# Two transformer blocks on one core: three column steps to one modulation step, the first mixer's norm directly behind its core, nine expert weights announced there

## The chip, the cores and the metric

The kernel runs on one core of one Trainium2 chip. The metric is the device time of one execution in microseconds, from the kernel's start to its end; several executions are timed and the median counts.

## The reference

`x` is 256 tokens by 1024 columns, `c` one row of 1024, all in float32. A first block mixes the tokens with two heads groups, then runs a mixture of experts; a second block follows (hybrid attention, two squared-ReLU MLPs, a pooling mixer). The change touches the first block, cut to what matters:

```python
mod = silu(c) @ ada_w + ada_b                       # 1024 x 6144
sh_m, sc_m, g_m, sh_f, sc_f, g_f = split(mod, 6)    # "modulation"
h = rms_norm(x, mix_norm_w) * (1 + sc_m) + sh_m
proj = h @ w_in                                     # "columns": r, k, v, lora, qk, v, o, gates
y_r = rwkv7(proj[..., :RWKV_COLS])                  # first mixer: a recurrence, then a norm per head
y_m = mlstm(proj[..., RWKV_COLS:])                  # second mixer: four heads, then a norm per head
x = x + g_m * (concat(y_r, y_m) @ w_out)
h = rms_norm(x, ffn_norm_w) * (1 + sc_f) + sh_f
x = x + g_f * moe(h)      # top group of 4, top 2 of its 8 experts; 32 experts x 3 weights of 1 MB
```

The second block starts with the same kind of modulation, from `c_2` and weights of its own.

## The kernel before

Activations lie with channels on the 128 partitions and 256 tokens along the row. A product is made of three fp32r matmuls, from a high and a low part of each operand; `split` makes the two parts of a weight, the high one on ScalarE, the low one on VectorE (line 297).

**Tiles.** Weights come through SyncE's DMA queue, in order, into 8 slots of 1 MB (tag `w`, `NWSLOT`). General work tiles of 128 x 1024 (tag `t4`) number 28 (`NT4`); three pairs `wh`/`wl` hold split weights (`NSPLIT`).

**Lanes.** The first block's work is laid out in program order by a small planner. Lane 0 holds the column products of `w_in` by name: `mg`, `r`, `v`, `mqk`, `mv`, `mo`, eight steps each apart from `mg`. Lane 1 holds the modulation loads of 1 MB each, eight a piece: `g1`, `f`, `ada00`, `gates20`, `ada01` (the last three belong to the second block). `side` is the second mixer as a generator, `mlstm_core`; it waits for `mqk` and `mv`, and asks for `mo` late. The first mixer is written straight through, `rwkv_prep`, `rwkv_core`, `rwkv_out`, and calls `fill(gap)` where TensorE would wait: one step of `side`, then steps of the lanes until the planned time `gap` is used up. A lane-1 step is taken when the planner thinks its load has come and `RATIO` lane-0 steps lie behind (line 208; `mg` and `r` go first). `need(names)` runs a lane up to a name, `more(n)` runs n lane-1 steps, `warm(n)` issues n matmuls of no use, which depend on nothing.

**Behind the core** (`run`, from line 2443): all columns and the rest of `side` are run to the end; then the gate of the first mixer, `rwkv_out` (the norm, with the half of the out projection that reads the second mixer, `pom`, as filler), ten expert loads (`E1`), `need("pom", "g1")`, the row of `g_m`, two expert loads, `need("f")`, the half of the out projection that reads the first mixer with the residual, four expert loads, then `route`. `route` runs three lane-1 steps (`R3`) and two more (`R6`), which are steps of `ada00`.

**Expert loads** (`moe_loads`, line 1738) are numbered n = 0 to 95: eight groups of four gate, four up and four down weights. The first 16 go ahead: n = 0 to 3 (from `WA`) into `w` slots, the next nine into pairs of `t4` tiles, three into the split pairs. n = 16 to 27 may take any of the three kinds that has come free, and from n = 28 (`REUSE`) only `w` slots. A load into `t4` or split tiles is two transfers of 0.5 MB, one into a `w` slot is one of 1 MB.

The program order is not the final order: the compiler's scheduler orders each engine's instructions by when it expects their operands and tiles, and that order is fixed then. On the chip each engine and each DMA queue works it off in order.

Of the kernel before, what the change touches and what calls it, by code (L numbers as in the profile page):

```python
# [45 lines left out]
SM, SO = 1, 1  # L46
PM, PO = "ada", "mm"
R1 = 0
RATIO = 2
R2 = 4  # L50
R3 = 3
R4 = 2
R5 = 0
R6 = 2
E5 = 3
GM = -1
VC = 2
WA = 0
EX = 1
CAT = (0, 1)  # L60
REUSE = 28
W1 = 4
W2 = 2
W3 = 0
# [5 lines left out]
W5 = 0  # L70
W6 = 0
N1 = 99
POS, E1, E2 = 10, 10, 2
BAND = 143

VEC_ROWS = [
# [77 lines left out]
class Net:  # L154
# [45 lines left out]

    def fill(self, gap):

        if self.side and next(self.side, None) is None:
            self.side = None
        end = self.now + gap
        while self.now < end:
            loaded = self.lanes[1] and self.vectors > 0 and self.arrival() + 2.0 <= self.now
            if self.lanes[0] and not (loaded and self.turns >= RATIO and self.lanes[0][0][0] not in self.urgent):
                self.step(0)
                self.turns += 1  # L210
            elif loaded:
                self.step(1)
                self.vectors -= 1
                self.turns = 0
            else:
                break
        self.now = max(self.now, end)

    def warm(self, n, after=None):

# [1288 lines left out]
    def route(self, ss, scale, shift):  # L1509
# [78 lines left out]
        B = small("Bm", 2, 32)  # L1588
        ohb = oh[:, :, :, None].to_broadcast([128, 2, 4, 8])
        nc.vector.tensor_mul(B.rearrange("p a (g e) -> p a g e", g=4), b8[:, :, None, :].to_broadcast([128, 2, 4, 8]), ohb)  # L1590
        self.more(R3)
        p = self.ps("ppos")
        self.mm(p[:, 0:32], self.c("striu"), B[:, 0], start=True, stop=True)
        self.mm(p[:, 32:64], self.ones, B[:, 0], start=False, stop=False, skip_group_check=True)
        self.mm(p[:, 32:64], self.c("striu"), B[:, 1], start=False, stop=True, skip_group_check=True)
        self.warm(R4)

# [9 lines left out]
        self.gather(S, 0)  # L1607
        self.more(R6)
        for _ in range(NWSLOT - 4):
# [128 lines left out]
    def moe_loads(self):  # L1738


        nc, I = self.nc, self.I
        self.moe_w = {}
        self.moe_free = {"w": NWSLOT, "t4": MOE_AHEAD - NSPLIT, "split": NSPLIT}
        for n, (kind, e) in enumerate(self.moe_order()):
            first = n < 4 + MOE_AHEAD
            order = ("w",) if WA <= n < WA + 4 else ("t4", "split") if first else ("w", "t4", "split") if n < REUSE else ("w",)
            while True:
                pool = next((o for o in order if self.moe_free[o]), None)
                self.stuck = pool is None
                if pool:  # L1750
                    break
                yield
            self.moe_free[pool] -= 1
            W = I["moe_w_" + kind][0, e]
            src = W.rearrange("(k p) n -> p k n", p=128) if kind == "down" else \
                W.rearrange("(h p j) n -> p h (j n)", h=1, j=8)
            if pool == "w":
                w = self.slot()
                if kind == "down" and e == 31:
                    for c in range(2):  # L1760
                        nc.sync.dma_start(w.rearrange("p (k c n) -> p k c n", k=2, c=2)[:, :, c],
                                          src.rearrange("p k (c n) -> p k c n", c=2)[:, :, c])
                elif kind == "down":
                    nc.sync.dma_start(w.rearrange("p (k n) -> p k n", k=2), src)
                else:
                    nc.sync.dma_start(w, src[:, 0])
                w = [w[:, 0:1024], w[:, 1024:2048]]
            else:
                if pool == "split":
                    w = [self.spool.tile([128, 1024], F32, name="we", tag=t) for t in ("wh", "wl")]  # L1770
                else:
                    w = [self.t4("we") for _ in range(2)]
                for h in range(2):
                    v = src[:, h] if kind == "down" else src[:, 0, h * 1024:(h + 1) * 1024]
                    nc.sync.dma_start(w[h], v)
            self.moe_w[kind, e] = (w, pool)
            yield
# [15 lines left out]
    def moe(self, S, consts):  # L1793
# [62 lines left out]
        for g in range(8):  # L1856
            if g == 2:
                self.overflow(S, gate, acc)
            p = self.ps("pgu")
            with self.behind(quad(g, 0, "gate", p)):  # L1860
                if last:
                    combine(g - 1, *last)
                self.slot_weights(S, g)
                if g in (5, 6):
                    residual(g - 5)
                if g == 7:
                    next(consts)
            ot, cwg = S["ot"], S["cwg"]
            with self.behind(quad(g, 1, "up", p)):
                t = act(p)  # L1870
                if g == 0:
                    self.overflow_flag(S)
                    gate = self.ada_gate(S["gate"], 1, "g_f")
                if g < 7:
                    self.gather(S, g + 1)
                if g == 5:
                    fw, fw2 = self.rows_of(self.vecs("final_norm_w"), "fw"), self.t4("fw2")
                    nc.scalar.activation(fw2, fw, AF.Square)
                last = ot, *down(g, t, cwg)
# [498 lines left out]
    def run(self):  # L2378
        nc, I = self.nc, self.I
# [6 lines left out]
        ss = self.ss()  # L2386
# [40 lines left out]
        M = {}  # L2427
# [15 lines left out]
        Y = self.rwkv_core(S)  # L2443
        self.mark("core")
        self.vectors = 99
        self.need("mg", "mqk", "mv", "mo")
        while self.side:
            self.fill(0)
        self.dump("ym", M["out"])
        self.expert_loads = self.moe_loads()  # L2450
        consts = self.attn_consts()

        def experts(n):
            for _ in range(n):
                next(self.expert_loads)

        HH, banks = [None, M["parts"]], {}
        self.later("pom", self.out_proj_half(I["w_out"][0], HH, 1, banks, True))
        S["gate"]()
        next(consts)  # L2460
        yr = self.rwkv_out(S, Y)
        self.dump("yr", yr)
        self.mark("out")
        experts(E1)
        HH[0] = self.split_act(yr)
        self.need("pom", "g1")
        self.gate = self.ada_gate(A["g1"]["m"], 0, "g_m")
        next(consts)
        experts(E2)
        self.need("f")  # L2470
        ss = self.ss()
        self.all(self.out_proj_half(I["w_out"][0], HH, 0, banks, False, ss))
        experts(4 + MOE_AHEAD - E1 - E2)
        self.dump_x("x1")
        mf = A["f"]["rows"]
# [24 lines left out]
        first = self.rsqrt(q, u)  # L2500
# [3 lines left out]
        for a in range(2):  # L2504
            n = [nc.vector.tensor_scalar(xn[a][:, 0:512], acc[a, 0], q[:, a:a + 1], None, op0=ALU.mult),
                 nc.scalar.activation(xn[a][:, 512:1024], acc[a, 1], AF.Copy, scale=q[:, a:a + 1])] if not XO else \
# [26 lines left out]
        HH = [None, self.split_act(osw)]  # L2533
        banks = {}
# [5 lines left out]
        ss = self.ss()  # L2540
# [10 lines left out]
        ss = self.ss()  # L2551
# [28 lines left out]
        ss = self.ss()  # L2580
# [5 lines left out]
        ss = self.ss()  # L2586
# [37 lines left out]
```

## Time and profile before

| | us |
|---|---|
| median of 3 timed runs | 1046.53 (1045.27 to 1047.58) |
| the profiled execution: its own time | 1038.73 |
| its span, from the first to the last instruction | 1037.1 |
| TensorE busy | 946.2 (91% of the span) |
| VectorE busy | 558.0 (54%) |
| ScalarE busy | 424.2 (41%) |
| GpSimd busy | 37.7 (4%) |
| TensorE's mean granted clock | 0.96 of full |
| read from HBM | 282.25 MB, with the writes 273 GB/s over the span |

The profile's page cuts the span into 40 slices of 25.9 us. Four stages can be told apart by the names of the matmuls: the first block's mixers to about 260 us, routing and experts to about 506, attention to about 650, then the two MLPs with the pooling mixer between them. A busy TensorE is not TensorE at its peak: the clock that it was granted has to be read beside it.

### The profile page before, as it was taken

The numbers are of one execution on the slowest core, as the hardware profiler recorded it, in microseconds if no ns is written. First come the engines' busy times: TensorE is split into PE (matmuls) and PEld (weight loads), VectorE is DVE, ScalarE is ACT, GpSimd is POOL, SyncE is SP. The second block draws the span as 40 slices with busy tenths as digits, with TensorE's granted clock in tenths as the row PEclk, the third lists the DMA queues.
The fourth block names the chain that finished last, engine by engine and source line by source line (L and its number), as shares of the span: only waits on it lengthen the run. The fifth ranks groups of instructions, "written<-read, shape, count | busy, mean of one in ns | idle before, by whom it ended". The sixth has DMA issues, their size and how long they took to land.

```text
span 1037.1 us, 18248 instructions
## 1 busy us (share of the span) xinstructions
PE 946.2 (91%) x7667; PEld 744.6 (72%) x7667; DVE 558.0 (54%) x941; ACT 424.2 (41%) x691; POOL 37.7 (4%) x53
## 2 busy tenths in 40 slices
PE   4898999989698877887899999999999999999996
PEld 1687776867474544444487677998989889999995
DVE  1477671536223221111499537898878775444446
ACT  1373334343212111021466435654444575444553
POOL 1020000001000000000000000100000010000000
PEclk9999999989689899898999999999999999999999
DMA  8998436537969999999995867799989925555501
GB/s 255 346 332 326 163 124 245 203 122 278 412 260 359 372 416 415 415 418 417 385 359 202 291 207 273 238 373 322 354 307 369 329 109 183 189 197 188 178 1 41
DMA packets 89658, 284.53 MB, mean 274 GB/s; under 512 B 10525, under 2 KB 14930, under 8 KB 77798
## 3 DMA queue, kind: packets, MB, share of 16 engines
q1 hardware_dynamic: 88106, 281.36, 73.5%
q10 hardware_dynamic: 956, 1.47, 0.4%
q8 instruction: 61, 1.00, 0.4%
q0 software_dynamic: 512, 0.52, 0.3%
q14 instruction: 23, 0.19, 0.0%
HBM read 282.25 MB, written 1.07 MB: 273 GB/s over the span
## 4 chain that ended last, share of the span: by engine, by line
PE 79%; DMA 10%; DVE 5%; ACT 3%; issue 2%; POOL 1%; SPq 1%; POOLq 0%; ACTq 0%; DVEq 0%
PE pB L181 28%; PE pm L181 17%; PE pgu L181 5%; DMA w<-in_moe_w_up_dram 4%; PE pada L457 4%; PE po L181 3%; DMA w<-in_moe_w_gate_dram 3%; PE pxg L181 3%; DMA w<-in_ada_w_dram 2%; PE pyd L181 2%; PE pacc L181 2%; PE pv L181 1%; DVE wl L297 1%; PE pgv L181 1%; DMA x<-in_x_dram 1%
## 5 line engine op out<-in xcount | busy, mean ns | idle before, releaser
L297 DVE TENSOR_TENSOR wl<-w,wh 128x1024 fp32r<-128x1024 f32 x186 | 226.9, 1225 | 124.3 <-ACT wh L296 124.2
L296 ACT CAST wh<-w 128x1024 fp32r<-128x1024 f32 x186 | 194.5, 1050 | 207.9 <-PE pB L181 98.8
L181 PE MATMUL pB<-hh,wh 128*128 128x256 f32 x800 | 219.1, 289 | 5.2 <-issue 2.8
L181 PE MATMUL pB<-hh,wl 128*128 128x256 f32 x800 | 215.7, 285 | 0.8 <-DVE wl L297 0.8
L181 PE MATMUL pB<-hl,wh 128*128 128x256 f32 x800 | 214.8, 285 | 0.8 <-DVE hl L657 0.7
L181 PEld LDWEIGHTS pB<-hh,wh 128*128 128x128 f32 x800 | 149.6, 193 | 16.6 <-issue 9.2
L181 PEld LDWEIGHTS pB<-hl,wh 128*128 128x128 f32 x800 | 149.1, 193 | 4.2 <-issue 2.9
L181 PEld LDWEIGHTS pB<-hh,wl 128*128 128x128 f32 x800 | 149.2, 193 | 3.7 <-issue 2.5
L181 PE MATMUL pm<-wh,fh 128*128 128x512 f32 (+1 forms) x262 | 101.2, 387 | 0.0
L181 PE MATMUL pm<-wl,fh 128*128 128x512 f32 (+1 forms) x262 | 100.8, 385 | 0.0
L181 PE MATMUL pm<-wh,fl 128*128 128x512 f32 (+1 forms) x262 | 100.6, 384 | 0.0
L181 PE MATMUL pgu<-w,xg 128*32 128x256 f32 x832 | 68.7, 440 | 23.3 <-DMA w<-in_moe_w_gate_dram 18.7
L181 PEld LDWEIGHTS pgu<-w,xg 128*32 128x32 f32 x832 | 31.6, 126 | 61.2 <-DMA w<-in_moe_w_gate_dram 26.2
L537 DVE SCALAR_TENSOR_TENSOR w<-w,csil 128x1024 f32<-128x1024 f32 x56 | 70.5, 1277 | 0.0
L181 PEld LDWEIGHTS pm<-wh,fh 128*128 128x128 f32 x262 | 49.1, 188 | 12.2 <-ACT fsq L2239 2.5
L181 PEld LDWEIGHTS pm<-wh,fl 128*128 128x128 f32 x262 | 49.2, 188 | 9.8
L181 PEld LDWEIGHTS pm<-wl,fh 128*128 128x128 f32 x262 | 49.3, 188 | 9.6 <-DVE wl L297 0.3
L457 PE MATMUL pada<-w,csil 128*32 128x512 f32 x256 | 43.6, 660 | 8.1 <-DMA w<-in_ada_w_dram 8.1
L2241 DVE TENSOR_TENSOR fl<-fsq,fh 128x512 fp32r<-128x512 f32 x32 | 22.0, 688 | 30.3 <-ACT fh L2240 30.3
L181 PE MATMUL pyd<-w,aT 128*32 128x512 f32 x224 | 28.9, 596 | 9.5 <-ACT aT L1819 9.5
L1654 ACT CAST slotT<-pcw 128x256 fp32r<-128x256 f32 x8 | 3.0, 373 | 78.4 <-PE pcw L181 78.4
L1625 DVE TENSOR_TENSOR oh<-cs,pos 128x256 f32<-128x256 f32 x8 | 3.4, 426 | 58.7 <-PE pcw L181 58.6
(556 smaller groups left out, 1291.0 us busy)
## 6 DMA issues: line engine op xcount, KB each, us to landing
w<-in_mlp_w_dram SPq DMA_DIRECT2D x64, 1024.0 KB
w<-in_ada_w_dram SPq DMA_DIRECT2D x40, 1024.0 KB
w<-in_ada_w_dram SPq DMA_DIRECT2D x64, 512.0 KB
w<-in_moe_w_up_dram SPq DMA_DIRECT2D x28, 1024.0 KB
w<-in_moe_w_down_dram SPq DMA_DIRECT2D x27, 1024.0 KB
w<-in_moe_w_gate_dram SPq DMA_DIRECT2D x24, 1024.0 KB
w<-in_w_in_dram SPq DMA_DIRECT2D x12, 1024.0 KB
w<-in_attn_w_in_dram SPq DMA_DIRECT2D x9, 1024.0 KB
```

What stands on the lines that cost most here:

```text
L181: return self.nc.tensor.matmul(out, lhsT, rhs, **kw)
L296: nc.scalar.copy(h, w)
L297: self.split_ins = nc.vector.tensor_sub(l, w, h)
L457: nc.tensor.matmul(acc[32 * j:32 * j + 32, :], self.csil[:, which, k:k + 1].to_broadcast([128, 32]), w[:, j * 512:(j + 1) * 512], start=(k ...
L537: nc.vector.scalar_tensor_tensor(acc[:, s], w[:, s], ck, acc[:, s], op0=ALU.mult, op1=ALU.add)
L1625: nc.vector.tensor_tensor(oh.rearrange("p a (e s) -> p a e s", s=32), self.c("slots")[:, None, None, :].to_broadcast([128, 2, 4, 32]), S[" ...
L1654: nc.scalar.copy(ot, p[:, 0:T])
L2241: nc.vector.tensor_sub(fl[:, s], sq[:, s], fh[:, s])
```

## The change

- `RATIO` goes from 2 to 3 until `mv` is done, and to 0 from then on. `fill` steps `side` once as before and then once more in every third round of its loop (new `side_step`).
- Behind the core nothing is run to its end any more. The gate, then nine expert loads (`E1` = 9), then `rwkv_out` follow at once. Only then comes `need("mo")`, and the half of the out projection that reads the first mixer is issued first, a step of it and a step of `side` by turns.
- `need("g1", "ada00")` stands ahead of the row of `g_m`; so all of `ada00` is done before the second half of the projection, which now reads the second mixer and carries the residual. Four expert loads (`E2`) stand between.
- In `route` the three and the two lane-1 steps are gone (`R6` = 0); 8 and 3 of the matmuls of no use stand in the places of `R3` and `R4`.
- `WA` = 9: the first nine expert loads go into `t4` pairs, the next four into `w` slots, three into split pairs.
- From group 2 on (`moe_big`) loads up to n = 83 (`LAST` = 84) may again take `t4` and split tiles.

```diff
--- before.py
+++ after.py
@@ -46,19 +46,19 @@
 SM, SO = 1, 1
 PM, PO = "ada", "mm"
 R1 = 0
-RATIO = 2
+RATIO = 3
 R2 = 4
-R3 = 3
-R4 = 2
+R3 = 8
+R4 = 3
 R5 = 0
-R6 = 2
+R6 = 0
 E5 = 3
 GM = -1
 VC = 2
-WA = 0
+WA = 9
 EX = 1
 CAT = (0, 1)
-REUSE = 28
+REUSE, LAST = 28, 84
 W1 = 4
 W2 = 2
 W3 = 0
@@ -70,7 +70,7 @@
 W5 = 0
 W6 = 0
 N1 = 99
-POS, E1, E2 = 10, 10, 2
+E1, E2 = 9, 4
 BAND = 143
 
 VEC_ROWS = [
@@ -200,12 +200,15 @@
 
     def fill(self, gap):
 
-        if self.side and next(self.side, None) is None:
-            self.side = None
         end = self.now + gap
+        self.side_step()
+        n, ratio = 0, 0 if "mv" in self.done else RATIO
         while self.now < end:
+            n += 1
+            if n % 3 == 0:
+                self.side_step()
             loaded = self.lanes[1] and self.vectors > 0 and self.arrival() + 2.0 <= self.now
-            if self.lanes[0] and not (loaded and self.turns >= RATIO and self.lanes[0][0][0] not in self.urgent):
+            if self.lanes[0] and not (loaded and self.turns >= ratio and self.lanes[0][0][0] not in self.urgent):
                 self.step(0)
                 self.turns += 1
             elif loaded:
@@ -215,6 +218,10 @@
             else:
                 break
         self.now = max(self.now, end)
+
+    def side_step(self):
+        if self.side and next(self.side, None) is None:
+            self.side = None
 
     def warm(self, n, after=None):
 
@@ -1588,7 +1595,7 @@
         B = small("Bm", 2, 32)
         ohb = oh[:, :, :, None].to_broadcast([128, 2, 4, 8])
         nc.vector.tensor_mul(B.rearrange("p a (g e) -> p a g e", g=4), b8[:, :, None, :].to_broadcast([128, 2, 4, 8]), ohb)
-        self.more(R3)
+        self.warm(R3)
         p = self.ps("ppos")
         self.mm(p[:, 0:32], self.c("striu"), B[:, 0], start=True, stop=True)
         self.mm(p[:, 32:64], self.ones, B[:, 0], start=False, stop=False, skip_group_check=True)
@@ -1740,10 +1747,11 @@
 
         nc, I = self.nc, self.I
         self.moe_w = {}
+        self.moe_big = False
         self.moe_free = {"w": NWSLOT, "t4": MOE_AHEAD - NSPLIT, "split": NSPLIT}
         for n, (kind, e) in enumerate(self.moe_order()):
             first = n < 4 + MOE_AHEAD
-            order = ("w",) if WA <= n < WA + 4 else ("t4", "split") if first else ("w", "t4", "split") if n < REUSE else ("w",)
+            order = ("w",) if WA <= n < WA + 4 else ("t4", "split") if first else ("w", "t4", "split") if n < REUSE or self.moe_big and n < LAST else ("w",)
             while True:
                 pool = next((o for o in order if self.moe_free[o]), None)
                 self.stuck = pool is None
@@ -1856,6 +1864,7 @@
         for g in range(8):
             if g == 2:
                 self.overflow(S, gate, acc)
+                self.moe_big = True
             p = self.ps("pgu")
             with self.behind(quad(g, 0, "gate", p)):
                 if last:
@@ -2443,33 +2452,35 @@
         Y = self.rwkv_core(S)
         self.mark("core")
         self.vectors = 99
-        self.need("mg", "mqk", "mv", "mo")
-        while self.side:
-            self.fill(0)
-        self.dump("ym", M["out"])
         self.expert_loads = self.moe_loads()
         consts = self.attn_consts()
 
         def experts(n):
             for _ in range(n):
                 next(self.expert_loads)
-
-        HH, banks = [None, M["parts"]], {}
-        self.later("pom", self.out_proj_half(I["w_out"][0], HH, 1, banks, True))
         S["gate"]()
+        experts(E1)
         next(consts)
         yr = self.rwkv_out(S, Y)
         self.dump("yr", yr)
         self.mark("out")
-        experts(E1)
-        HH[0] = self.split_act(yr)
-        self.need("pom", "g1")
+
+        HH, banks = [self.split_act(yr), None], {}
+        self.need("mo")
+        po = self.out_proj_half(I["w_out"][0], HH, 0, banks, True)
+        while self.side:
+            next(po, None)
+            self.side_step()
+        self.all(po)
+        self.dump("ym", M["out"])
+        HH[1] = M["parts"]
+        self.need("g1", "ada00")
         self.gate = self.ada_gate(A["g1"]["m"], 0, "g_m")
         next(consts)
         experts(E2)
         self.need("f")
         ss = self.ss()
-        self.all(self.out_proj_half(I["w_out"][0], HH, 0, banks, False, ss))
+        self.all(self.out_proj_half(I["w_out"][0], HH, 1, banks, False, ss))
         experts(4 + MOE_AHEAD - E1 - E2)
         self.dump_x("x1")
         mf = A["f"]["rows"]
```

## Rows read from the trace of the kernel before

**Rows 1.** The page: GB/s of all DMA in 40 slices of the span

```profile
GB/s 255 346 332 326 163 124 245 203 122 278 412 260 359 372 416 415 415 418 417 385 359 202 291 207 273 238 373 322 354 307 369 329 109 183 189 197 188 178 1 41
```

**Rows 2.** Chain that ended last, whole span: start us, us, what

```profile
358.62 12.88 DMA w<-in_moe_w_up_dram
...
477.78 14.36 DMA w<-in_moe_w_up_dram
```

**Rows 3.** Windows: length; busy PE, PEld, DVE, ACT, POOL; PEclk; DMA share, GB/s

```profile
210.00:240.00 30.00, 27.23 (x150) 19.52 (x149) 11.15 (x23) 11.48 (x20) 5.76 (x5) 0.83 0.30 106
240.00:260.00 20.00, 19.79 (x115) 15.20 (x114) 15.96 (x31) 7.74 (x14) 1.86 (x3) 1.00 0.97 374
260.00:270.00 10.00, 1.86 (x7) 0.49 (x5) 2.11 (x5) 1.22 (x5) 1.60 (x2) 0.75 1.02 413
270.00:290.00 20.00, 18.51 (x74) 14.83 (x74) 5.64 (x34) 4.13 (x8) 0.43 (x2) 0.50 0.92 365
290.00:300.00 10.00, 9.19 (x99) 6.19 (x102) 2.64 (x9) 1.51 (x4) 0.00 (x0) 0.88 0.40 154
...
320.00:350.00 30.00, 25.76 (x298) 17.03 (x297) 7.01 (x19) 4.52 (x11) 0.00 (x0) 0.94 0.84 331
...
370.00:480.00 110.00, 86.04 (x778) 47.25 (x778) 22.30 (x51) 16.61 (x38) 0.00 (x0) 0.92 1.02 416
```

**Rows 4.** Windows of 10 us, same columns

```profile
200.00:210.00 10.00, 10.00 (x128) 8.71 (x127) 6.86 (x24) 3.78 (x6) 0.73 (x1) 1.00 0.49 190
...
230.00:240.00 10.00, 10.00 (x55) 8.55 (x54) 2.70 (x5) 3.56 (x5) 3.59 (x3) 1.00 0.01 2
```

**Rows 5.** Timeline of SyncE's queue, 160 to 282: start us, us, issue

```profile
185.95 17.54 SPq L1766 DMA_DIRECT2D w<-in_moe_w_gate_dram  x4
...
217.83 22.17 SPq L445 DMA_DIRECT2D w<-in_ada_w_dram  x2
240.06 4.77 SPq L1775 DMA_DIRECT2D we<-in_moe_w_up_dram  x8
246.44 9.86 SPq L1775 DMA_DIRECT2D we<-in_moe_w_down_dram  x8
257.25 0.33 SPq L445 DMA_DIRECT2D w<-in_ada_w_dram  x1
```

**Rows 6.** Waits of SyncE's queue, 200 to 300: us, times, longest

```profile
SPq L445 <- DVE wl L297: 21.5, 1, 21.5
```

**Rows 7.** Timeline of TensorE, routing: start us, us, group, count [idle before <-releaser]

```profile
259.82 0.28 PE L181 MATMUL po<-wh,yl 128*128 128x256 f32 x1
...
268.69 1.91 PE L457 MATMUL pada<-w,csil 128*32 128x512 f32 x2 [8.14 <-DMA w<-in_ada_w_dram]
...
281.71 1.93 PE L457 MATMUL pada<-w,csil 128*32 128x512 f32 x6
...
287.63 6.07 PE L181 MATMUL pxg<-oh,xp 128*128 128x128 f32 x32
293.62 1.92 PE L457 MATMUL pada<-w,csil 128*32 128x512 f32 x16
...
296.95 3.23 PE L181 MATMUL pgu<-w,xg 128*32 128x256 f32 x56
```

**Rows 8.** Timeline of TensorE, from the core's end to the projection

```profile
210.23 0.68 PE L181 MATMUL pyi<-Pm,Z 64*64 64x64 f32 x16
...
223.18 2.15 PE L436 MATMUL pbc<-cs,rb 128*128 128x128 f32 x8 [1.99 <-DVE rb L431]
...
228.04 1.88 PE L181 MATMUL pc<-Y,first 128*128 128x512 f32 x4
...
248.78 0.50 PE L181 MATMUL po<-wh,yh 128*128 128x512 f32 x1
```

**Rows 9.** Chain that ended last, a later gather

```profile
347.97 3.78 PE pxg L181 x32
...
353.60 3.76 PE pyd L181 x32
```

## The prediction

> **What bounds the kernel now.** I read the chain that ended last first, then the busy time by windows, then the queue of SyncE and TensorE's timeline where the chain names them.
>
> In the experts' stage the chain is held five times by an expert weight's transfer, 12.5 to 15.5 us each, 69.8 us together [rows 2]. The page shows why: the transfers run at 415 to 418 GB/s in five slices on end [rows 1], and 416 over 110 us [rows 3]. No window shows clearly more for long, so this stage ends when its bytes are in. It can end earlier only if bytes move before it.
>
> Before it they could. From 210 to 300 us five windows move 106 x 30 + 374 x 20 + 413 x 10 + 365 x 20 + 154 x 10 = 23.6 MB [rows 3]; at 416 GB/s that is 56.8 us, so 33.2 us of transfer time are lost. The worst stretch is 230 to 240 with 2 GB/s [rows 4]. SyncE's queue says what it waited for: four gate weights took slots from 186 to 203, and a modulation load then sat 21.5 us until a split freed a slot [rows 5, 6]. The twelve loads into work tiles stood behind it in the queue and came at 240 [rows 5].
>
> Their late start hits back in routing. A load of `ada00` issued at 257.25 queues behind sixteen halves of expert weights, and TensorE, whose fixed order has this step between two transposes, stands 8.14 us until 268.69 [rows 5, 7]. The granted clock is 0.50 over the next 20 us [rows 3], which is its lower level, 1.2 of 2.4 GHz.
>
> In the core itself there is little to win: TensorE is busy 10.00 of 10 us from 200 to 210 at full clock [rows 4].
>
> **Part by part.**
>
> *The three lane-1 steps in `route` go.* They are the groups at 268.69, 281.71 and 293.62 [rows 7]. (1) The stall: 8.1 us. (2) The first step itself, 1.9 us at half clock. (3) The last one: the gather ends at 293.7, the experts' first matmul starts at 296.95, 3.25 us later; in a later group the same pair is 1.85 us apart (351.75 to 353.60) [rows 9]. Gain 1.4 us. (4) The gather itself took 6.07 us, and 3.78 at a better clock [rows 7, 9]: 2.3 us, or nothing if the clock falls all the same. (5) From 270.6 to 281.2 lie transposes and router products at half clock, 10.6 us; between nothing and 5.3 us; I take 3, since part of it waits for copies. The middle step (281.71, 1.93 us) lies beside VectorE's top-k and costs nothing now. Sum 16.7 us, between 11.4 (without 4 and 5) and 19.0.
>
> *The matmuls of no use*, 8 and 3, stand where TensorE waits for VectorE (from 283.6, where the step of 281.71 ends, to the next product); they depend on nothing and cost 0, at most the 1 us by which eight of them outlast that wait at half clock, which I leave in the range.
>
> *The three steps come earlier*, 16 matmuls of two steps took 1.92 us [rows 7], so 2.9 us more before the projection's second half. Their loads move with them, ahead of the split-pair loads on SyncE's queue.
>
> *The norm directly behind the core.* Now TensorE waits there for the second mixer's norm (1.99 us at 223.18 [rows 8]); from 210 to 240 it is idle 2.8 us, and at a mean clock of 0.83 about 10.2 us run at the lower level [rows 3]. Full cover gains at most 2.8 + (10.2 - 2.8) / 2 = 6.5 us. Against it: the norm's chain, from 228.04 to the first product with its result at 248.78, is 20.7 us long [rows 8], and now one half of the projection runs under it. A half is 11.3 us (248.78 to 260.1 [rows 7, 8]). In the change both halves follow the chain, and under it lie the rest of `mo`, of the modulation (eight steps of 0.96 us for `ada00` alone) and the last of the second mixer. With the 2.9 us, the bounds are a gain of 6.5 - 2.9 = 3.6 and a loss of 11.3 - 3.6 = 7.7. TensorE's work is the same in sum, and the planner kept it at 10.00 of 10 with the same fillers [rows 4], which is nearer the good end; I take 0.
>
> *Ratio 3, then 0, and more steps of `side`.* The order changes, the sum of the work does not, and TensorE is full either way [rows 4]. 0, and what shifts here is inside the bounds above.
>
> *Nine loads announced at the core, none in a slot.* They need no weight slot, so neither they nor the slots' users wait as at 217.83 [rows 5]. They cost TensorE nothing and SyncE 18 issues of 0.33 us. The price of being late or early is in the transfers: if the experts start 16.7 us earlier, the same 23.6 MB must come in 73.3 us, 322 GB/s. The windows at 240 to 270 show 374 and 413 [rows 3], so there is room.
>
> *Work tiles and split tiles reused up to n = 83.* At full rate deeper buffers give nothing. From 320 to 350 the rate is 331 [rows 3], and this is 30 x (1 - 331 / 416) = 6.1 us of transfer time; most of it lies before group 2. 0 to 2.5, I take 1. Against this part speaks what the Trainium skill says in "DMA: Bandwidth & Descriptors", Rules for kernel authors: transfers of at least 1 MiB for full bandwidth, and these loads are cut in two. By the fit in its section on the anatomy of one DMA (2.0 us and the bytes over 436 GB/s, given for GpSimd's path) two halves would take 6.4 us and a whole 4.4; an estimate for 56 loads with nothing overlapped is 112 us more, and the sum would be a loss. Here eight halves were issued in 9.86 us [rows 5] while the windows, filled with such halves, moved 374 and 413 GB/s [rows 3]. The trace disagrees with the rule, since the fixed part overlaps, and I give it no chance of its own.
>
> **Sum.** 16.7 + 0 + 1 = 17.7 us, taken one to one from the end of the experts' stage, since it is bound by transfers that start that much earlier, and from there to the end, where TensorE's work is unchanged. The profiled span 1037.1 becomes 1019.4; its own time of 1038.73 lies 7.8 below the median of 1046.53, and I carry the difference over: 1046.5 - 17.7 = 1028.8. The terms' bounds give a gain of 3.7 to 25.1, the lost transfer time of 33.2 us is the outer limit.
>
> **The rivals.**
>
> *The norm is held by tiles.* Nine loads are eighteen of 28 work tiles, asked for ahead of the norm's own. Where the second mixer and `mo` still hold theirs, the norm waits, its chain starts where it does now, and a whole half of the projection comes uncovered behind it: 11.3 us back, a gain of 6.4, 1040.1. For it: the twelve loads came only at 240. Against: the wait named there is for a weight slot [rows 6].
>
> *The wait for `ada00` moves.* Its last loads queue behind nine expert weights, and TensorE stands ahead of the projection's second half instead of in routing. The stall, the step and the half clock come back there: 8.1 + 1.9 + 3 + 2.3 = 15.3 us, a gain of 2.4, 1044.1. For it: this is what happened at 257.25 behind the same loads [rows 5]. Against: the slots are free, so the loads can be issued sooner.
>
> *The transfers give it all back.* The experts start earlier, but the loads before do not come earlier, and the chain's waits of 12.5 to 15.5 us grow by as much: no change, 1046.5. For it: the stage is bound by bytes [rows 2]. Against: 230 to 240 at 2 GB/s [rows 4] was for want of slots.
>
> *Slower: the queue is blocked in the experts' stage.* With up to n = 83 on work and split tiles, SyncE's fixed order puts loads for different tiles in one line; a load whose tile comes free late holds those whose slots are free, and the rate falls. At the 331 GB/s of 320 to 350 the bytes of the 110 us from 370 to 480 take 138.2 us [rows 3]: 28.2 us more, 1057. It decides from 358 GB/s down, where the loss is 17.7. Against: up to twenty buffers instead of eight.
>
> **How the numbers follow.** The forecast has 0.55, tiles 0.15, `ada00` 0.12, given back 0.08, blocked queue 0.10. A measurement of this kernel can tell about 0.2% from no change, 2.1 us. Faster: 0.55 + 0.15, half of the 0.12 and a little of the 0.08, 0.78; within: 0.10; slower: 0.10 and a little, 0.12. The range leaves out the blocked queue and what is given back, and reaches from the forecast's best bound with some of the 33.2 us beyond it, 1016, to the moved wait, 1045.
>
> **What would show it.** No modulation matmul between the projection's last product and the experts' first, and about 20 us between these two instead of 37.1. The clock in routing above 0.8. A first load into work tiles at about 212 and over 300 GB/s from 215 to 240. The experts' first product at about 280, their last at about 489, with five waits still near 14 us. If the first load into work tiles is still near 240, or the norm's first product near 228, the tiles hold it; a wait for a modulation load ahead of the row of `g_m` is the second rival; a rate under 400 in the middle of the experts' stage is the slower one. I am wrong altogether if the core itself ends at another time than now (its last product stands at 210.23 [rows 8]), since I gave its new order nothing.

## The result: 1.1% slower

The changed kernel takes 1057.99 us (median, 1055.03 to 1058.87), the kernel before 1046.3 beside it: a ratio of 1.0106, interval [1.0083, 1.0129]. The forecast was 1028.8. The profiled execution of the changed kernel took 1057.74 us, span 1056.1, so the two traces lie 19.0 us apart, and the readings below add up to 19.0. Some 7 of these are no cost of the change: the trace of before is of an execution 7.8 us quicker than its median, as the prediction says.

| us from the span's start, TensorE | before | after | later by |
|---|---|---|---|
| first mixer's core, begin of its last product group | 210.23 | 229.81 | 19.6 |
| norm's first product `pc` | 228.04 | 232.25 | 4.2 |
| first projection product with the norm's result | 248.78 | 263.40 | 14.6 |
| begin of the last projection product | 259.82 | 291.92 | 32.1 |
| first expert product | 296.95 | 310.46 | 13.5 |
| end of the last expert product | 508.03 | 521.24 | 13.2 |
| end of TensorE's last product | 1029.11 | 1048.14 | 19.0 |

So the routing does what was forecast: from the last projection product to the first expert product it takes 18.5 us instead of 37.1. Everything ahead of it is 32.1 us late, and the attention behind the experts loses another 5.8: from the last expert product to the first product of the first MLP it is 168.0 us instead of 162.2.

The line numbers of after are those of before plus 7 from about line 220 on and plus 8 from about 1750 on; in the other kernels they shift by other amounts, and the names tell what is meant. TensorE's timeline of after from the core's end to the experts, for [rows 7, 8] (start us, us, group, count, idle before and releaser):

```profile
220.02 0.68 PE L181 MATMUL pyi<-Pm,Z 64*64 64x64 f32 x16
...
229.81 0.68 PE L181 MATMUL pyi<-Pm,Z 64*64 64x64 f32 x16
...
234.06 6.21 PE L464 MATMUL pada<-w,csil 128*32 128x512 f32 x56
240.21 1.09 PE L443 MATMUL pbc<-cs,rb 128*128 128x128 f32 x8
...
256.52 1.11 PE L443 MATMUL pbc<-cs,rb 128*128 128x128 f32 x4 [10.35 <-DVE rb L438]
261.53 1.11 PE L443 MATMUL pbc<-cs,rb 128*128 128x128 f32 x4 [3.90 <-DVE rb L438]
263.40 0.79 PE L181 MATMUL po<-wh,yh 128*128 128x512 f32 x1 [0.75 <-ACT yh L1223]
...
291.92 0.28 PE L181 MATMUL po<-wh,yl 128*128 128x256 f32 x1
...
305.10 5.43 PE L181 MATMUL pxg<-oh,xp 128*128 128x128 f32 x32 [0.32 <-DVE b L1621]
310.46 1.91 PE L181 MATMUL pgu<-we,xg 128*32 128x256 f32 x29
```

Two things stand out. Between the core's last two products (220.02, 229.81) lies nearly 9 us of other work: 71 products `pB` in single rows, the second mixer's projection `mo`, which its core asks for with `need("mo")` in the middle of the first mixer's chain. And the norm's `pbc` products wait 10.35 and 3.90 us for a copy `rb`. VectorE's timeline of after says what that copy stood behind:

```profile
226.05 0.75 DVE L542 TENSOR_SCALAR w<-w,csil 128x1024 f32<-128x1024 f32 x1 [2.96 <-DMA w<-in_ada_w_dram]
...
253.42 1.28 DVE L544 SCALAR_TENSOR_TENSOR w<-w,csil 128x1024 f32<-128x1024 f32 x1 [8.43 <-DMA w<-in_ada_w_dram]
...
256.04 0.42 DVE L438 COPY rb<-hr 128x512 f32<-128x512 f32 x1
256.37 1.28 DVE L544 SCALAR_TENSOR_TENSOR w<-w,csil 128x1024 f32<-128x1024 f32 x1
...
261.05 0.42 DVE L438 COPY rb<-hr 128x512 f32<-128x512 f32 x1
```

Lines 542 and 544 are the running sum of `gates20`, a modulation that only the attention wants, some 300 us later. The planner, at none to one, has begun it, and its product at 253.42 waits 8.43 us for its load. The copy's own input is there by about 247, when GpSimd's `hr` ends. The load of `gates20` is behind 18 halves of expert weights on SyncE's queue, whose timeline answers to [rows 5]:

```profile
223.19 4.47 SPq L1783 DMA_DIRECT2D we<-in_moe_w_gate_dram  x8
229.10 10.63 SPq L1783 DMA_DIRECT2D we<-in_moe_w_up_dram  x8
240.69 1.62 SPq L1783 DMA_DIRECT2D we<-in_moe_w_down_dram  x2
243.25 4.09 SPq L452 DMA_DIRECT2D w<-in_ada_w_dram  x4
248.34 1.66 SPq L728 DMA_DIRECT2D w<-in_w_out_dram  x2
```

The windows of after, for [rows 3, 4] (length; busy PE, PEld, DVE, ACT, POOL; PEclk; DMA share, GB/s):

```profile
230.00:240.00 10.00, 10.00 (x84) 4.26 (x80) 2.77 (x7) 4.03 (x9) 0.00 (x0) 1.00 1.02 411
...
250.00:260.00 10.00, 1.11 (x4) 0.71 (x4) 6.57 (x11) 0.00 (x1) 0.00 (x0) 0.50 1.03 398
...
320.00:330.00 10.00, 9.54 (x106) 6.22 (x109) 3.50 (x8) 4.00 (x9) 0.00 (x0) 1.00 0.35 120
...
370.00:480.00 110.00, 73.23 (x723) 41.96 (x724) 19.23 (x47) 14.35 (x32) 0.00 (x0) 0.83 1.02 412
```

The transfers did come early, 411 GB/s at 230 to 240 where there had been 2. But from 250 to 260 TensorE works 1.11 of 10 us, and at 320 to 330, in the midst of the experts, the transfers fall to 120 GB/s, where before they had 294.

### The profile page after: what moved, and what is told of

It is laid out like the page before. It is cut to its first block, busy times and chain, and to the rows that moved or that the text cites. A ratio compares the mean times of both kernels' runs of the same rounds, so it can differ in the third digit from the quotient of the medians.

```text
span 1056.1 us, 18325 instructions
## 1 busy us (share of the span) xinstructions
PE 935.5 (89%) x7676; PEld 744.7 (71%) x7676; DVE 560.5 (53%) x941; ACT 423.4 (40%) x691; POOL 37.4 (4%) x53
## 4 chain that ended last, share of the span: by engine, by line
PE 50%; DMA 10%; DVE 2%; issue 2%; ACT 1%; POOL 0%; SPq 0%; POOLq 0%; ACTq 0%; DVEq 0%
PE pB L181 20%; PE pm L181 16%; PE pgu L181 3%; DMA we<-in_moe_w_up_dram 2%; PE po L181 2%; DMA we<-in_moe_w_gate_dram 2%; DMA w<-in_moe_w_gate_dram 2%; DMA w<-in_moe_w_up_dram 1%; PE pyd L181 1%; DMA w<-in_moe_w_down_dram 1%; PE pgv L181 1%; DMA w<-in_ada_w_dram 1%; DMA we<-in_moe_w_down_dram 1%; PE pacc L181 1%; PE pada L464 1%
## 5 line engine op out<-in xcount | busy, mean ns | idle before, releaser
L181 PE MATMUL pgu<-w,xg 128*32 128x256 f32 x528 | 39.8, 416 | 27.9 <-DMA w<-in_moe_w_gate_dram 25.6
L181 PEld LDWEIGHTS pgu<-w,xg 128*32 128x32 f32 x528 | 19.6, 120 | 48.1 <-DMA w<-in_moe_w_gate_dram 27.4
L464 PE MATMUL pada<-w,csil 128*32 128x512 f32 x256 | 38.0, 661 | 0.0
L1840 DVE SCALAR_TENSOR_TENSOR mg<-pyd,slotw,g_f 128x512 f32<-128x512 f32 x16 | 12.0, 749 | 45.6 <-PE pyd L181 42.5
L181 PEld LDWEIGHTS pxg<-oh,xp 128*128 128x128 f32 x256 | 30.8, 201 | 3.2 <-issue 2.5
```

Of the source, the lines that this page charges most:

```text
L181: return self.nc.tensor.matmul(out, lhsT, rhs, **kw)
L464: nc.tensor.matmul(acc[32 * j:32 * j + 32, :], self.csil[:, which, k:k + 1].to_broadcast([128, 32]), w[:, j * 512:(j + 1) * 512], start=(k ...
L1840: nc.vector.scalar_tensor_tensor(yg[:, s], py[c], cwg, gate[:, s], op0=ALU.mult, op1=ALU.mult)
```

## The experiments

From here every run is compared with runs of the kernel before on its own chip, by ratio: there before had medians of 1043.8, 1043.7 and 1041.8 us, and single executions between 1035.1 and 1049.0. "MB issued" is added up from SyncE's queue; the expert weights are 100.7 MB in all. The theories were these. A: the planner's new order makes the first mixer's core late. B: the early `gates20` holds the norm on VectorE. C: the early expert weights do, on SyncE's queue. D: none to one goes on in the attention. E: a begun `gates20` keeps a weight slot through the experts' stage. F: what the early expert weights take is large slots, and `ada00` lacks them.

### The two halves of the change alone

`e3_planner_only`, on the kernel before:

```
-RATIO = 2
+RATIO = 3
...  fill(): the changed one, with n % 3 and ratio 0 behind "mv"
```

> The kernel before with the new planner alone (three to one, then none to one once the second mixer's v columns are done; its core stepped at every third step): tail, routing and loads as before. Theory A: the core ends about 20 us later; the second mixer's steps that stood between core and norm (17.8 us from 210.23 to 228.04) are gone, so the net is +2 to +10 us, and with gates20 ahead of the norm up to +20: 1049 to 1066 us. Rival (the planner helps and the tail is at fault): 1030 to 1043 us.

Measured: 1073.94 us, ratio 1.0312 [1.0259, 1.0365], worse than A's upper end. The core ends 14 us late and the experts begin 13 us late, their stage takes another 12 us more, and from there to the end it is 6 us more.

`e4_routing_only`, on the kernel before:

```
-R3 = 3
-R4 = 2
+R3 = 8
+R4 = 3
...
-R6 = 2
+R6 = 0
...
-        self.more(R3)
+        self.warm(R3)
...
-        self.need("pom", "g1")
+        self.need("pom", "g1", "ada00")
```

> The kernel before with the routing part alone: ada00 is finished ahead of the first gate, the five modulation steps in the routing become eight warming products there, none at its end. The sum of the prediction for this part: -16.7 us, 1029.8 us, with the stretch from the last projection product to the first expert product at about 20 us instead of 37.1. Rival 1 (the 47 us of ada00's steps move ahead of the second projection half and cost there what they cost here): 1040 to 1046 us. Rival 2 (the experts' stage is bound by its loads at 416 GB/s, which do not start earlier): the first expert product comes 15 us earlier, the last one at the same time, 1044 to 1047 us.

Measured: 1039.29 us, ratio 0.9970 [0.9946, 0.9995], 3.1 us. That is Rival 1, 0.7 us below its range. The routing is some 17 us long, and ahead of it TensorE's timeline shows the stall that was taken out of it:

```profile
259.63 1.94 PE L457 MATMUL pada<-w,csil 128*32 128x512 f32 x8 [15.72 <-DMA w<-in_ada_w_dram]
...
294.96 3.66 PE L181 MATMUL pgu<-w,xg 128*32 128x256 f32 x64
```

The step that in routing waited 8.14 us [rows 7] waits 15.72 us ahead of the first gate, and the experts begin 2 us earlier than before. So moving the steps is worth next to nothing as long as their loads come when they come.

### Where the planner's loss lies

`e1_gates_late`, on the changed kernel:

```
-            loaded = self.lanes[1] and self.vectors > 0 and ...
+            loaded = self.lanes[1] and self.lanes[1][0][0] not in self.held and self.vectors > 0 and ...
...
-        R["gate"] = A["g1"]["m"]
+        R["gate"], self.held = A["g1"]["m"], ()
```

with `held` at first `("gates20", "ada01")`.

> The changed kernel, in which the two later modulations gates20 and ada01 may not start before the routing is done. Theory B (VectorE's queue: the products of gates20 wait for their loads and hold the norm's small copies rb behind them): the two TensorE gaps of 10.35 and 3.90 us ahead of the norm's pbc go, the first projection product moves from 263.4 us to 249-254 us, and of the 5.7 us lost in the attention stage some come back: 1038 to 1046 us. Theory C (the nine early expert weights fill SyncE's queue and hold the loads that the norm's neighbours need): the gaps stay under another name, 1055 to 1060 us. By either the core ends where it does in the changed kernel, 229.8 us.

Measured: 1045.73 us, ratio 1.0019 [0.9990, 1.0049]; the changed kernel had 1.0106. For the norm B holds. TensorE's timeline:

```profile
243.46 1.06 PE L443 MATMUL pbc<-cs,rb 128*128 128x128 f32 x4
244.91 1.12 PE L443 MATMUL pbc<-cs,rb 128*128 128x128 f32 x4 [0.39 <-DVE rb L438]
249.12 0.80 PE L181 MATMUL po<-wh,yh 128*128 128x512 f32 x1 [3.09 <-ACT yh L1223]
```

The gaps of 10.35 and 3.90 us are 0 and 0.39, and the projection starts at 249.12 instead of 263.40. But its last product begins at 287.91 instead of 291.92: of 14.3 us only 4.0 are left, and 2.5 of these come from a core that ends earlier (last product group at 227.31). The rest went where C said, to the loads. TensorE's timeline, ScalarE's and that of SyncE's queue:

```profile
272.57 0.79 PE L181 MATMUL po<-wh,yh 128*128 128x512 f32 x1 [8.82 <-ACT wh L303]
```

```profile
271.48 1.99 ACT L303 CAST wh<-w 128x1024 fp32r<-128x1024 f32 x2 [16.21 <-DMA w<-in_w_out_dram]
```

```profile
247.06 1.62 SPq L1783 DMA_DIRECT2D we<-in_moe_w_down_dram  x2
249.62 2.93 SPq L1772 DMA_DIRECT2D w<-in_moe_w_down_dram  x3
253.47 0.34 SPq L1774 DMA_DIRECT2D w<-in_moe_w_gate_dram  x1
254.75 3.92 SPq L728 DMA_DIRECT2D w<-in_w_out_dram  x2
```

The weights of the projection's second half are asked for behind nine expert weights in halves and four whole ones, and TensorE waits 8.82 us for them. So C holds for the projection, as far as the place in the queue shows it; this planner with fewer early weights was not run.

The experts' stage is 8 us shorter too (202.5 us for 210.8). What I had not seen right is the attention: from the last expert product to the end the time grew, from 526.9 to 530.2 us.

`e5_attention_ratio` is that kernel with the ratio set back to 2 behind the routing:

```
-        n, ratio = 0, 0 if "mv" in self.done else RATIO
+        n, ratio = 0, self.after or (0 if "mv" in self.done else RATIO)
...
+        R["gate"], self.held, self.after = A["g1"]["m"], (), 2
```

> As e1_gates_late, and behind the routing the planner goes by two column steps to one of modulation again, as in the kernel before (in the changed kernel its ratio of none to one stays for the rest of the program, since the second mixer's v columns stay done). Theory D (that ratio puts modulation steps, whose weights are only being loaded then, ahead of the attention's own products): the stretch from the last expert product to the end, 530.2 us in e1_gates_late, 521.1 us in the kernel before, is back at 520-523 us, and the time falls by 7 to 10 us to 1034-1040. Rival (the attention is longer because gates20 and ada01, 16.8 MB, are loaded there): it stays at 528-531 us and 1043-1048 us. The kernel before loads 16.8 MB there too, which speaks for D.

Measured: 1038.02 us, ratio 0.9954 [0.9923, 0.9986]. From the last expert product to the end it is 519.9 us again: D. The windows of the same 20 us of the attention, first of `e1_gates_late`, then of `e5_attention_ratio`:

```profile
548.00:568.00 20.00, 14.74 (x87) 10.41 (x88) 17.13 (x47) 9.04 (x27) 0.53 (x1) 0.74 0.87 317
```

```profile
546.00:566.00 20.00, 18.20 (x108) 14.65 (x108) 19.91 (x60) 14.68 (x42) 0.62 (x1) 1.00 0.45 161
```

With none to one, modulation is ahead of the attention's own work while its weights still come in (317 GB/s), and TensorE works 14.74 of 20 us at a granted clock of 0.74.

The core's own 19.6 us were parted by two kernels of which one execution each was timed. `e8_ratio_stays_3`, on the changed kernel:

```
-        n, ratio = 0, 0 if "mv" in self.done else RATIO
+        n, ratio = 0, RATIO
```

> The changed kernel with three column steps to one of modulation throughout, never none to one. gates20 isn't begun ahead of the routing by this order. The lateness of the core (19.6 us at its last product) is parted in two: what comes of none to one (the 34 modulation products ahead of pm, some 5 us, and the sums behind them) goes, what comes of three to one and of stepping the second mixer inside the gaps stays. Theory A1 (the second half is the larger): last core product at 222 to 227 us. Theory A2 (none to one is the larger): 211 to 218 us. The time falls with the core and the free weight slot by 12 to 25 us to 1033-1046.

`e11_side_once`, on the changed kernel:

```
-            n += 1
-            if n % 3 == 0:
-                self.side_step()
```

> The changed kernel with the second mixer's core stepped once at the start of each gap, as before, and not at every third step; three to one and then none to one stay. The core's last product, 230.5 us in the changed kernel and 221.8 us without none to one, tells what the stepping is worth: theory A1 (three to one and the second mixer's steps in the gaps): 220 to 226 us; theory A3 (the stepping costs nothing, the ratios are everything): 229 to 231 us. gates20 is begun early here too, so the experts' loads stay at 380 to 395 GB/s; the time is 1045 to 1060 us.

Measured: the core's last product group in `e8_ratio_stays_3` (1043.29 us) and then in `e11_side_once` (1056.35 us), from TensorE's timelines:

```profile
221.07 0.68 PE L181 MATMUL pyi<-Pm,Z 64*64 64x64 f32 x16
```

```profile
209.20 0.68 PE L181 MATMUL pyi<-Pm,Z 64*64 64x64 f32 x16
```

229.81 with both, 221.07 without none to one, 209.20 without the stepping: where before stands, 210.23. All stated ranges are missed, A1 in `e8_ratio_stays_3` narrowly: the ratios alone cost the core nothing, the stepping at three to one some 11 us, and stepping and none to one together 19.6. In `e8_ratio_stays_3` the 96 products of `mo` come in eight groups of 12, the last from 215.27 on; in the changed kernel 25 come in smaller pieces, and `need("mo")` pays for 71 at once, 8.7 us, which is the difference between the two.

The other 11 us are not only work put between the chain's products. The windows from 85 to 205 us, of before, after, `e8_ratio_stays_3` and `e11_side_once`:

```profile
85.00:205.00 120.00, 116.81 (x1719) 88.87 (x1719) 64.80 (x145) 42.29 (x68) 1.46 (x2) 0.97 0.57 205
```

```profile
85.00:205.00 120.00, 112.27 (x1532) 86.89 (x1535) 61.00 (x129) 37.67 (x64) 5.10 (x4) 0.91 0.49 178
```

```profile
85.00:205.00 120.00, 112.77 (x1537) 90.14 (x1536) 62.02 (x128) 38.76 (x65) 4.66 (x4) 0.93 0.48 172
```

```profile
85.00:205.00 120.00, 113.97 (x1706) 86.12 (x1708) 63.83 (x149) 39.88 (x67) 1.64 (x2) 0.96 0.56 199
```

With the stepping TensorE is idle some 4 us longer (112.77 for 116.81 of 120), and its granted clock is 0.93 instead of 0.97, which by these rows is at most 0.04 x 120 = 4.8 us: together up to 9 of the 11, an estimate. Whether the stepping lowers the clock by way of this idle time was not tried; the five traces with it have 0.91 to 0.93 here, the others that were read 0.96 to 1.00.

Yet the core's lateness is not the kernel's: with the core on time, `e11_side_once` has a ratio of 1.014 in its one execution, no better than the changed kernel. Its experts begin at 301.28, 9.2 us ahead of the changed kernel, of 20.6 at the core; their stage is as long (210.8 us), and from there to the end it takes 534.7 us instead of 526.9. I had expected the core to carry the loss, and the modulations carry at least as much of it.

### The slot that a begun modulation keeps

`e2_old_planner`, on the changed kernel:

```
-RATIO = 3
+RATIO = 2
...  fill(): that of before
-E1, E2 = 9, 4
+E1, E2 = 4, 4
```

> The changed kernel with the planner of before (two column steps to one of modulation, the second mixer's core stepped once per gap), and with four expert weights instead of nine announced ahead of the norm, because nine do not fit beside this order. Theory A (the planner's order alone makes the core late): the core's last product is back at about 210 us from 229.8, and the time falls by 15 to 20 us to 1038-1043. Rival (the second mixer's steps have to run somewhere; without the new planner they stand behind the core again): the core is back at 210 us, but the second mixer's projection and core take 10 to 20 us behind it, 1047 to 1058 us.

Measured: 1041.06 us, ratio 0.9986 [0.9957, 1.0014], inside A's range. The core is back at 211.2 and the experts begin at 292.7, 4.2 us ahead of before. Then their stage takes 223.3 us instead of 211.1, and the gain is gone. Here the transfers have a hole, which `e6_old_planner_gates_late` closes with the bar of `e1_gates_late` on top:

> As e2_old_planner (the planner of before, four weights ahead of the norm), with gates20 and ada01 barred until the routing is done. In e2_old_planner the experts' loads, 78.2 MB still to issue at the first expert product, took 209.6 us (373 GB/s; 411 in the kernel before), and a begun gates20 keeps one weight slot as its running sum through the whole stage. Theory E (that slot is what the loads lack): 78 MB at 411 GB/s, 190 us, 15 to 20 us less: 1022 to 1030 us. Rival (the four and nine weights in other tile pools cause the holes in the loads): the stage stays at 205-212 us and the time within 4 us of e2_old_planner, 1037 to 1045 us.

Measured: 1023.14 us, ratio 0.9791 [0.9731, 0.9851]: E. The window 300 to 310 of `e2_old_planner`, and what SyncE's queue waits for there (us in all, times, longest):

```profile
300.00:310.00 10.00, 9.54 (x98) 6.71 (x93) 3.29 (x9) 3.34 (x9) 0.00 (x0) 1.00 0.01 2
```

```profile
SPq L1771 <- PE pyd L181: 26.4, 1, 26.4
```

and the same window of `e6_old_planner_gates_late`:

```profile
300.00:310.00 10.00, 9.54 (x102) 6.36 (x104) 3.51 (x8) 3.67 (x9) 0.00 (x0) 1.00 0.83 315
```

`gates20` multiplies into a weight slot and keeps it until the attention. One of eight slots less, and a load of an up weight waits 26.4 us for the first expert to free one, with loads into free work tiles behind it on the queue: 2 GB/s against 315. From the first expert product to the last issue 78.1 MB took 209.6 us in the one (373 GB/s) and 76.0 MB 185.8 in the other (409). In the changed kernel the same wait is 13.2 us and the window is the one with 120 GB/s.

### What the early weights are worth, and where

`e7_old_planner_nine` is `e6_old_planner_gates_late` with nine weights announced, the first four in large slots as in before:

```
-WA = 9
+WA = 0
...
-E1, E2 = 4, 4
+E1, E2 = 9, 4
```

> As e6_old_planner_gates_late, but nine expert weights announced ahead of the norm, the first four of them in the large slots as in the kernel before (with the changed choice of slots nine do not fit). If early loads are worth what they weigh: some 2 to 3 MB more issued by the first expert product, 5 to 7 us less than e6_old_planner_gates_late. If they only stand ahead of ada00's and the projection's loads on SyncE's queue: the first projection product comes 5 to 15 us later and the time is the same or up to 10 us more.

`e10_four_large` is `e6_old_planner_gates_late` with only the first of these two edits:

> As e6_old_planner_gates_late (1023.1 us) with one number changed: the first four expert weights take large slots, as in the kernel before. It parts the two differences between e6_old_planner_gates_late and e7_old_planner_nine (1034.7 us). Theory F (the slots): ada00 is late again and the time is 1031 to 1038 us. Rival (the number of weights ahead of the norm, nine or four): 1021 to 1027 us.

`e12_six` is `e6_old_planner_gates_late` with `E1 = 6`:

> As e6_old_planner_gates_late with six expert weights instead of four announced ahead of the norm. If weights announced early are worth what they weigh: 2 to 4 us less than 1023.1. If they stand ahead of the projection's loads on SyncE's queue: first projection product 3 to 8 us later than 237.1, and the time 1024 to 1032 us. If the slots decide when they are loaded, and not the place of their announcement: within 2 us.

Measured: nine with large slots 1034.74 us, 0.9923 [0.9885, 0.9960]; four with large slots 1041.98, 0.9988 [0.9961, 1.0016]; six without 1021.48, 0.9824 [0.9767, 0.9881]; four without 0.9791 from above. The number is worth nothing between four and six and some 0.6% between four and nine; which slots the first four take is worth 2%. Of the expectations, that of `e12_six` holds in its third form, within 2 us. `e7_old_planner_nine` fits neither of its own: the projection is not later (237.17 for 237.11), and the time is 12 us more. `e10_four_large` is on F's side and beyond its range. SyncE's queue with four weights, not in large slots (`e6_old_planner_gates_late`), then in large slots (`e10_four_large`):

```profile
156.29 43.37 SPq L449 DMA_DIRECT2D w<-in_ada_w_dram  x10
199.70 4.84 SPq L1780 DMA_DIRECT2D we<-in_moe_w_gate_dram  x8
```

```profile
163.53 12.41 SPq L1771 DMA_DIRECT2D w<-in_moe_w_gate_dram  x4
180.87 42.71 SPq L449 DMA_DIRECT2D w<-in_ada_w_dram  x8
224.11 8.29 SPq L725 DMA_DIRECT2D w<-in_w_out_dram  x4
246.51 12.74 SPq L1771 DMA_DIRECT2D w<-in_moe_w_up_dram  x3
259.30 4.75 SPq L1780 DMA_DIRECT2D we<-in_moe_w_up_dram  x8
```

Without the four in the slots all of `ada00` is issued by 200 us, and weights go to work tiles at once. With them `ada00` ends at 224 and the first loads into work tiles are at 259. F's own wait is the smaller part of the price: TensorE waits 3.9 us for `ada00` in `e10_four_large`. Its experts begin 5.4 us later than in `e6_old_planner_gates_late`, and their stage takes 211.6 us instead of 203.8, with the weights coming later.

The last run asks whether this needs the new tail at all. `e9_slots_only` is `e4_routing_only` with one number more, on the kernel before:

```
-WA = 0
+WA = 9
```

> As e4_routing_only (kernel before with the routing part; 1039.3 us, ada00's last steps waited for their loads ahead of the first gate and gave the 18 us back), and in addition the first four expert weights no longer take large slots; the ninth to twelfth do. Theory F (in the kernel before the four early expert weights and two projection halves hold the large slots from 163 to 203 us, so ada00's loads come late; where they don't, ada00 is done with the core and the routing's gain stays): the first expert product at 278 to 287 us from 295.0, the time 1025 to 1032 us. Rival (the tail's order is what makes room for ada00, the slots alone do nothing, or the later loads cost the experts as much): 1036 to 1043 us.

Measured: 1022.57 us, ratio 0.9818 [0.9778, 0.9858]: F, and better than its range. SyncE's queue and TensorE's timeline of it:

```profile
182.92 0.38 SPq L1764 DMA_DIRECT2D w<-in_moe_w_down_dram  x1
184.43 28.14 SPq L445 DMA_DIRECT2D w<-in_ada_w_dram  x5
```

```profile
238.76 1.92 PE L457 MATMUL pada<-w,csil 128*32 128x512 f32 x14
...
276.74 1.50 PE L181 MATMUL pgu<-we,xg 128*32 128x256 f32 x24
```

No wait is left at `pada`. The experts begin at 276.74, 20.2 us ahead of before, and end at 492.98, 15.1 ahead. The last load of `ada00` is issued at 212; in `e4_routing_only` it was 248.21, behind the weights, and the same routing part gave 3 us.

In sum the parts fit. The planner alone is 1.0312, routing and slots without it 0.9818; their product is 1.0124, and the changed kernel measured 1.0106 [1.0083, 1.0129]. For the tail's new order and the reuse up to n = 83 together nothing is left that these runs can tell from zero: `e9_slots_only` with the old tail and without the reuse and `e12_six` with both have the same ratio. By stage they are not alike. In `e12_six` the experts begin at 284.95, 8.2 us later, and their stage takes 203.1 us instead of 216.2. Why it is shorter was not tried: less is left to issue at its start (76.0 MB for 78.1), and only `e12_six` has the reuse.

## Why the prediction was wrong

**The step that failed** is *Ratio 3, then 0, and more steps of `side`*, put at 0 with "the sum of the work does not [change], and TensorE is full either way". It costs 3.1% by itself (`e3_planner_only`), and the second half of that sentence did not hold. In the changed kernel it shows in four places. The core ends 19.6 us late, by the lump of `mo` (8.7) and by the stepping, with which TensorE works less and at a lower clock already from 85 to 205 us. A modulation is begun that nobody wants yet, and TensorE is idle for 14.3 us at the norm behind VectorE, an engine that the step did not look at. The same modulation keeps a weight slot, 8 us of the experts' stage. And the ratio stays for the rest of the program: 5.8 us in the attention, 9 in `e1_gates_late`. The prediction did say that another end of the core would make it wrong altogether; it did not ask what the planner would do where there is no column work left.

**The routing term** of 16.7 us was right as a mechanism and in size: 18.6 us shorter in the changed kernel, and without the planner 20.2 us at the first expert product. Of its fourth part, 2.3 us for the gather, the changed kernel got 0.6 (5.43 us for 6.07). The forecast's experts' first product at about 280 and last at 489 are nearly what `e9_slots_only` shows, 276.74 and 492.98. "One to one from the end of the experts' stage" was too much by a quarter there, 15.1 of 20.2 us.

**The second rival**, that the wait for `ada00` moves, had the right price (a gain of 2.4 us left; `e4_routing_only` gained 3.1, with a stall of 15.72 us) and the wrong cause. I let the nine announced weights decide it; the four in large slots do. The nine have their price elsewhere, where *Nine loads announced at the core* had none for TensorE: the wait of 8.82 us for the projection's weights in `e1_gates_late`. The words "none in a slot" stand in the prediction as an argument against a cost, and they were the larger part of the gain: on top of the routing they bring 1.5%, and the routing without them 0.3%. In the changed kernel `ada00` came in time by another way as well, since none to one drew its steps ahead of the projection; there it was paid for in the core and behind it.

**The norm behind the core**, put at 0 between a gain of 3.6 and a loss of 7.7, came out at the bad end. From the core's last product group to the last projection product it is 49.6 us before, and 51.6 in `e9_slots_only`, which keeps the old tail. With the new tail and the planner of before it is 56.7 (`e6_old_planner_gates_late`) and 57.0 (`e12_six`), a loss of about 7. In the changed kernel it is 62.1, beyond the bound, which was worked out from TensorE alone and knows neither VectorE's queue nor SyncE's.

**The slower rival** named a blocked queue in the experts' stage with a rate below 358 GB/s. A blocked queue there is (waits of 26.4 and 13.2 us), though the rate over the stage of `e2_old_planner` falls to 373 only, and its reason is the slot of `gates20`, not the reuse up to n = 83, which `e6_old_planner_gates_late` has as well. That its 1057 lies 1 us from the measured 1058 is luck: in the changed kernel the transfers ran at 412 GB/s from 370 to 480, and the experts' stage is as long as before (210.8 us for 211.1). What the reuse is worth stays open, as it was not tried alone.

## What to carry to other kernels

A planner's rule is judged by what it draws forward when its first choice runs out, on every engine and in every later stage, and not by whether the engine it fills is full. Work begun early holds what it has begun with: a slot, a place in VectorE's order, a place in the load queue. Before a wait is moved, ask what the load behind it waits for; one number that freed its slot was worth five times the move. And count what a removed wait gave back at the end of the stage, not where it stood: of 14.3 us at the norm 4.0 were left behind the projection.

## What the runs showed of the chip that I had not expected

A copy of 0.42 us on VectorE, ready but behind a product that waited 8.43 us for its load, kept TensorE idle for 10.35 us. The granted clock was 0.50, the lower level, from 250 to 260, where TensorE worked 1.11 of 10 us. It was 1.00 again from 270 to 290, behind 7.72 of 10 us from 260 to 270, and TensorE was busy 18.76 of 20 us there.

From 370 to 480 us the transfers ran at 416 GB/s before, with whole weights, and at 412 in the changed kernel, with halves among them. The three windows of 2, 2 and 120 GB/s (before at 230 to 240, `e2_old_planner` at 300 to 310, after at 320 to 330) each had a load at the head of SyncE's queue that waited for a tile, 21.5, 26.4 and 13.2 us.
